# Four neighbouring tokens in a group: the layout of a routed-weight table, the stores that feed its stage, and the weights of the value pass

## The chip, the cores and the metric

The kernel runs on one core of a Trainium2 chip. The metric is the device time of one execution in microseconds, smaller is better. Matrix products run on TensorE (PE in the profile; PEld is its weight load), copies and element-wise work on VectorE (DVE), ScalarE (ACT) and GpSimd (POOL); SyncE (SP) only issues transfers.

## The reference, cut to what matters

A decoder block: attention and convolution side by side, a layer norm, and then an expert mixer in which the change lies. Each of 256 tokens has 8 heads that each pick 16 of 16,384 experts. An expert is one row of a table u and one row of a table v, 2048 numbers each:

```python
def block(yb):                      # PEER_BLOCK = 128 tokens
    ...                             # top-k over product keys: eidx [b, t, h, 16]
    g = jax.nn.softmax(top.astype(jnp.float32), axis=-1)
    u = u_tab[eidx]
    v = v_tab[eidx]
    h = jax.nn.gelu(jnp.einsum('btd,bthkd->bthk', yb, u))
    return jnp.einsum('bthk,bthkd->btd', g * h, v).astype(y.dtype)
```

The result is scaled, added to the residual and normalised once more.

## The kernel before, in words

The mixer does not gather all the rows. It computes the dot products of all tokens with all experts as matrix products over most of the columns (the other columns are gathered row by row), picks out the routed ones, and turns the routed weights back into a full matrix for a second matrix product.

- **The table W** is [128, 256, 128] fp32 in SBUF: partition p, token t, block j, for expert 128 j + p.
- **The u pass** (about 485 to 967 us) loops over 128 blocks. SP loads 128 rows of u (`u_load`, L1195), PE transposes them (ut, L1223), ScalarE and VectorE split them into a high and a low part (uh L1226, ul L1227), and PE adds three products (hi by hi, lo by hi, hi by lo: `mm3`, L290 to L292) into hp. ScalarE writes hp to W[:, :, j] (`u_keep`, L1474). Between these blocks run the `steps` of the routing, one or two pieces in each turn of the loop. The last of them is `feature_steps`: it forms features of the two key numbers (i1 and i2) of each routed slot, and stores them in bf16 to DRAM (feat, L1508). Each store goes out on ScalarE's queue, so it stands among the uh of the loop.
- **The x stage** (about 967 to 1148 us) works on groups of four tokens, 64 of them. Group q is the four tokens 32 apart, `group(t, q)`. The features of a group are loaded (L1545, L1554); small matmuls turn them into one-hot masks; `ext` (L1627) picks the 128 routed values of each token from W; GELU and the gates follow; and `sc` (L1674) makes, for each token, a 128 x 128 matmul that scatters the gated weights over partitions and blocks. The four matmuls of a group fill one PSUM bank, one quarter each, and `sc_keep` (L1682 on ScalarE, L1680 on VectorE) copies it over the group's part of W. Up to group 36 one group is scattered in each step, afterwards two in each.
- **The v pass** (about 1148 to 1645 us) loops over the 128 blocks j. W[:, :, j] is the weight matrix (stationary) and 1408 columns of the 128 rows of v are the moving matrix. Both are split into high and low parts: wh on ScalarE (L1720) and wl on VectorE (L1721), for two blocks at a time; vh (L1731) and vl (L1732) block by block. For each block PE makes 18 matmuls (`v_part`): three column pieces of 512, 512 and 384, two tiles of 128 tokens, and the three products of `mm3`. The other 640 columns are gathered for each token's own experts (gv, L1697 on GpSimd) and added up by VectorE (gacc, L1702).

Each engine works through its own list in order. The order of the x stage is written out by hand; that of the u and v pass follows the order of the calls. Each transfer that SP or ScalarE starts signals one of eight semaphores, in turn (DMAHW0 to DMAHW7), and waits for the transfer that used the semaphore before, unless that is known to have ended.

Of the kernel before, what the change touches and what calls it, by code (L numbers as in the profile page):

```python
# [9 lines left out]
F32R = mybir.dt.float32r  # L10
# [3 lines left out]
AF = mybir.ActivationFunctionType  # L14
# [5 lines left out]
P = 128  # L20
T = 256
# [54 lines left out]
def tile_hybrid_block(  # L76
# [6 lines left out]
    nc = tc.nc  # L83
    x, w_in, w_out, wq = x[0], w_in[0], w_out[0], wq[0]
# [3 lines left out]
    def dump(name, ap):  # L88
        if name in dbg:
            nc.sync.dma_start(dbg[name], ap)  # L90

    def flat3(t, a, b):
        return t[:, : a * b].rearrange("p (a b) -> p a b", b=b)
# [31 lines left out]
    raws, parts = {}, {}  # L125
# [163 lines left out]
    def mm3(acc, ah, al, bh, bl, start, stop):  # L289
        nc.tensor.matmul(acc, lhsT=ah, rhs=bh, start=start, stop=False)  # L290
        nc.tensor.matmul(acc, lhsT=ah, rhs=bl, start=False, stop=False)  # L291
        nc.tensor.matmul(acc, lhsT=al, rhs=bh, start=False, stop=stop)  # L292
# [650 lines left out]
    if True:  # L943
# [25 lines left out]
        for s in range(2):  # L969
            hi, lo = (stream.tile([P, 1024], F32R, name=f"{n}0_{'ab'[s]}", tag=n, bufs=HLB) for n in ("hi", "lo"))  # L970
            w = slice(s * 512, s * 512 + 512)
# [7 lines left out]
        for u in range(2):  # L979
            split_to(u)  # L980
            for j in range(4):
                i = j if u else (0, 2, 1, 3)[j]
# [139 lines left out]
    def gate_softmax(tt):  # L1122
        sh = [P, PH, TOPK]
        nc.vector.tensor_tensor(gs[:, tt], top[:, tt], top[:, tt, :, 0:1].to_broadcast(sh), op=OP.subtract)
        nc.scalar.activation(gs[:, tt], gs[:, tt], AF.Exp)
        nc.vector.tensor_reduce(gsum[:, tt, :, 0], gs[:, tt], axis=AX.X, op=OP.add)
        nc.vector.reciprocal(gsum[:, tt], gsum[:, tt])
        nc.vector.tensor_tensor(gs[:, tt], gs[:, tt], gsum[:, tt].to_broadcast(sh), op=OP.mult)

    def fl(t, tt):  # L1130
        return t[:, tt].rearrange("p a b -> p (a b)")
# [185 lines left out]
    if True:  # L1317
# [7 lines left out]
        i = nphase + 6  # L1325
# [41 lines left out]
        i = first_wq  # L1367
# [24 lines left out]
        for h in range(1, PH):  # L1392
            for half in range(2):
                p = 2 * h + half
# [37 lines left out]
        sp = scores.pop(PH - 1)  # L1432
# [22 lines left out]
    wpool = ctx.enter_context(ExitStack())  # L1455
    wp = wpool.enter_context(tc.tile_pool(name="wp", bufs=1, reuse_waits="tile"))
    W = wp.tile([P, T, P], F32, name="W")
    gbs = ctx.enter_context(ExitStack())
    rings.append([gbs.enter_context(tc.tile_pool(name="gb", bufs=GMORE, reuse_waits="tile")), GMORE, 0])
    wT, wv = gs.rearrange("p a b c -> p (a b c)"), hv  # L1460
    gT, ha = (t.rearrange("p a b c -> p (a b c)") for t in (i1, top))
    feats = [dram.tile([2, 5, P, P], BF, name=f"feat{n}") for n in range(2)]
# [10 lines left out]
    def u_keep(j):  # L1473
        nc.scalar.activation(W[:, :, j], hps.pop(j), AF.Copy)  # L1474

# [4 lines left out]
    def feature_steps():  # L1480
        dump("i1", i1)
        dump("i2", i2)
        for n, src in enumerate((i1, i2)):

            size = BIGM if n == 0 else 1.0
            v = src.rearrange("p a b c -> p a (b c)")
            sqf = tk.tile([P, 2, P], F32, name=f"fsq{n}", tag="oh", bufs=1)
            nc.vector.tensor_tensor(sqf, v, v, op=OP.mult)
            sqi = tk.tile([P, 2, P], U32, name=f"fsi{n}", tag="cand", bufs=1)
            nc.vector.tensor_copy(sqi, sqf)  # L1490
            yield
            for f in range(4):
                fr = tk.tile([P, 2, P], BF, name=f"fr{n}{f}", tag="scr", bufs=4)
                if f == 0:
                    nc.vector.memset(fr, size)
                elif f == 1:
                    nc.vector.tensor_scalar(fr, v, size, None, op0=OP.mult)
                else:
                    si = tk.tile([P, 2, P], U32, name=f"fi{n}{f}", tag="oh", bufs=1)
                    if f == 2:  # L1500
                        nc.vector.tensor_scalar(si, sqi, 7, 7, op0=OP.logical_shift_right,
                                                op1=OP.logical_shift_left)
                    else:
                        nc.vector.tensor_scalar(si, sqi, 127, None, op0=OP.bitwise_and)
                    nc.vector.tensor_scalar(fr, si, size, None, op0=OP.mult)
                yield
                for r in ((0, 1) if f == 0 else (f + 1,)):
                    nc.scalar.dma_start(feats[n][:, r].rearrange("a p c -> p a c"), fr)  # L1508
        for tt in range(2):
            gate_softmax(tt)  # L1510
            yield
        pt = psu.tile([P, 512], F32, name="colsg", tag="ut", bufs=4)
        for tt in range(2):
            nc.tensor.transpose(pt[:, tt * P:(tt + 1) * P], fl(gs, tt), ident)
        nc.scalar.activation(gT, pt[:, :T], AF.Copy)
        yield
# [13 lines left out]
        yield from feature_steps()  # L1530

    def group(t, q):
        tt, b = divmod(q, 32)
        return t[:, tt * P + b:(tt + 1) * P:32]

    NB = 4
    frow, bts = {}, {}
# [86 lines left out]
    def ext(q):  # L1624
        hot, wq_ = pts.pop(q), group(W, q)
        for j in range(4):
            nc.tensor.matmul(xps[q][:, j * P:(j + 1) * P], lhsT=hot[:, j], rhs=wq_[:, j],  # L1627
                             start=False, stop=j == 3)

    def ext_max(q):  # L1630
        nc.vector.tensor_reduce(group(ha, q), flat3(xps.pop(q), 4, P), axis=AX.X, op=OP.max)
# [32 lines left out]
    def sc_val(m, pair=False):  # L1664
        oas[m] = flat3((slots_[5], *more_slots, slots_[4], slots_[6])[m % 4] if pair else slots_[5 + m % 2], 4, P)
        ww, pp = group(wT, m), pos.pop(m)[1]
        wb = ww.rearrange("p (j o) -> p j o", o=1).to_broadcast([P, 4, P])
        nc.vector.scalar_tensor_tensor(oas[m], flat3(pp, 4, P), 0.0, wb, op0=OP.is_equal, op1=OP.mult)

    def sc(m, pair=False):  # L1670
        sp = (banks[4:6] + more_banks)[m % 4] if pair else banks[5]
        oh, oa = ohs.pop(m), oas.pop(m)
        for j in range(4):
            nc.tensor.matmul(sp[:, j * P:(j + 1) * P], lhsT=oh[:, j * P:(j + 1) * P], rhs=oa[:, j],  # L1674
                             start=True, stop=True)
        return sp

    def sc_keep(m, sp, vector=False):
        if vector:
            nc.vector.tensor_copy(group(W, m), flat3(sp, 4, P))  # L1680
        else:
            nc.scalar.activation(group(W, m), flat3(sp, 4, P), AF.Copy)  # L1682

    psv = ctx.enter_context(ExitStack())

# [1 line left out]
    raws, parts = {}, {}  # L1687
# [23 lines left out]
    nb = len(blocks)  # L1711
    halves_ = {}

    def v_rows(p, tt):
        if p not in halves_:
            halves_[p] = [vps[p % 2].tile([P, T, 2], F32R, name=f"w{x}{p}", tag=f"w{x}") for x in "hl"]
        s = slice(0, T) if tt is None else slice(tt * P, tt * P + P)
        wh, wl = (t[:, s] for t in halves_[p])
        src = W[:, s, 2 * p:2 * p + 2]
        nc.scalar.activation(wh, src, AF.Copy)  # L1720
        nc.vector.tensor_tensor(wl, src, wh.bitcast(F32), op=OP.subtract)  # L1721

    def v_cols(j, s, early=False):
        src, vhl = raws[j], parts.setdefault(j, [])
        if not vhl:
            vhl.extend(vps[j % 2].tile([P, VC], F32R, name=f"v{x}{j}", tag=f"v{x}") for x in "hl")
        vh, vl = (t[:, s] for t in vhl)
        if early:
            nc.gpsimd.tensor_copy(vh, src[:, s])
        else:  # L1730
            nc.scalar.activation(vh, src[:, s], AF.Copy)  # L1731
        (nc.gpsimd if early else nc.vector).tensor_tensor(vl, src[:, s], vh.bitcast(F32), op=OP.subtract)  # L1732

    def v_split(j):
        if j % 2 == 0:
            v_rows(j // 2, None)
        v_cols(j, slice(0, VC))

    def ahead_jobs():
# [72 lines left out]
    if True:  # L1812
# [41 lines left out]
        for q in range(QP, NQ + 1):  # L1854
            m = q - LAG
# [30 lines left out]
            if m >= 0:  # L1886
                sc_keep(m, sc(m))
# [4 lines left out]
        for m in range(NQ - QP, NQ, 2):  # L1892
# [12 lines left out]
            for p, sp in zip((m, m + 1), sps):  # L1905
                sc_keep(p, sp, p % 2 == 1)
            if m == NQ - 12:
                v_raw(2)
                v_rows(0, 0)
# [5 lines left out]
            if m == NQ - QP + 2:  # L1915
# [5 lines left out]
                vps = [psv.enter_context(tc.tile_pool(name="vp0", bufs=1, reuse_waits="tile", side="right"))]  # L1921
# [6 lines left out]
    if stop == "u":  # L1928
        dump("hv", hv)
        if "H" in dbg:  # L1930
            nc.sync.dma_start(dbg["H"], W)
        return
# [4 lines left out]
    acc = [[psv_.tile([P, 512], F32, name=f"f{tt}{b}", tag=f"f{tt}{b}")[:, :e - a]  # L1937
            for b, (a, e) in enumerate(blocks)]
           for tt in range(2)]
# [4 lines left out]
                v_sum(j, tt, nc.vector)  # L1944

    def v_part(j, tt, b, stop=False):
        (wh, wl), vhl = halves_[j // 2], parts[j]
        (a, e), s = blocks[b], slice(tt * P, tt * P + P)
        mm3(acc[tt][b], wh[:, s, j % 2], wl[:, s, j % 2], vhl[0][:, a:e], vhl[1][:, a:e], j == 0, stop)

    def v_use(j, tts=range(2)):
        for b in range(nb):
            for tt in tts:
                v_part(j, tt, b)
# [11 lines left out]
    if True:  # L1966
        v_rows(0, 1)
        for j in range(P):
# [7 lines left out]
            elif len(z2) < 2:  # L1976
                tt = len(z2)
# [113 lines left out]
```

## Time and profile before

| | |
|---|---|
| median of 3 runs | 1669.9 us |
| lowest to highest | 1668.81 to 1670.19 us |
| the profiled execution | 1661.9 us |
| its span in the profile | 1660.1 us |
| mean granted TensorE clock | 0.993 |
| TensorE busy | 1621.2 us, 98% of the span |
| VectorE, GpSimd, ScalarE busy | 87%, 53%, 49% |
| transfers | 475.19 MB, mean 286 GB/s |

Times inside the profile are in microseconds from the start of the span. A row of the groups gives line, engine, operation, tiles and shape, the count, then busy time, the mean of one in ns, and the idle time ahead of it with what ended it. A row of the timeline gives start, length and the instruction; ACTq and SPq are the queues on which ScalarE and SyncE issue transfers. A matmul's length holds its way through the array, so the distance of two starts tells how long the array is taken by one.

### The profile page before, as it was taken

The numbers are of one execution on the slowest core, as the hardware profiler recorded it, in microseconds if no ns is written. First come the engines' busy times: TensorE is split into PE (matmuls) and PEld (weight loads), VectorE is DVE, ScalarE is ACT, GpSimd is POOL, SyncE is SP. The second block draws the span as 40 slices with busy tenths as digits, with TensorE's granted clock in tenths as the row PEclk, the third lists the DMA queues.
The fourth block names the chain that finished last, engine by engine and source line by source line (L and its number), as shares of the span: only waits on it lengthen the run. The fifth ranks groups of instructions, "written<-read, shape, count | busy, mean of one in ns | idle before, by whom it ended". The sixth has DMA issues, their size and how long they took to land.

```text
span 1660.1 us, 30619 instructions
## 1 busy us (share of the span) xinstructions
PE 1621.2 (98%) x11627; PEld 1499.5 (90%) x11627; DVE 1451.2 (87%) x2660; ACT 812.9 (49%) x1260; POOL 887.0 (53%) x653
## 2 busy tenths in 40 slices
PE   9999999999999999999999999989999999999996
PEld 8998989988999999999999997878888888888884
DVE  6999667756899999999999879978889899898998
ACT  4444766645334444444444546867444444444442
POOL 0885000064573333333333347857887877777773
PEclk9999999999999999999999999999999999999998
DMA  9774435366658999999999988765999999999997
GB/s 286 228 230 142 154 111 189 102 222 197 215 186 313 353 349 351 350 353 344 352 348 354 360 314 270 253 208 183 336 363 365 349 354 348 351 350 353 350 352 263
DMA packets 178349, 475.19 MB, mean 286 GB/s; under 512 B 18305, under 2 KB 86425, under 8 KB 177945
## 3 DMA queue, kind: packets, MB, share of 16 engines
q1 hardware_dynamic: 117188, 253.62, 45.0%
q0 software_dynamic: 57488, 218.66, 35.9%
q8 instruction: 91, 1.49, 0.4%
q10 hardware_dynamic: 3524, 0.95, 0.2%
q14 instruction: 58, 0.47, 0.1%
HBM read 468.32 MB, written 4.85 MB: 285 GB/s over the span
## 4 chain that ended last, share of the span: by engine, by line
PE 54%; POOL 18%; issue 12%; DVE 9%; DMA 4%; ACT 2%; POOLq 0%; DVEq 0%; SPq 0%; ACTq 0%
POOL gv L1697 16%; PE hp L292 6%; PE hp L290 6%; PE hp L291 6%; PE ut L1223 6%; PE bank L1674 3%; DMA gv<-in_peer_v_dram,e 2%; DVE taps L483 2%; PE bank L1627 2%; PE pwq L292 1%; PE pwq L291 1%; PE pwq L290 1%; DVE gu L1166 1%; PE mixa L290 1%; PE pq L290 1%
## 5 line engine op out<-in xcount | busy, mean ns | idle before, releaser
L1697 POOL DMA_INDIRECT gv<-in_peer_v_dram,e x256 | 397.1, 1551 | 109.4 <-DVE gacc L1702 65.2
L1155 POOL DMA_INDIRECT gu<-in_peer_u_dram,eu x206 | 195.5, 949 | 318.2 <-DVE gu L1166 224.7
L290 PE MATMUL hp<-yh,uh 128*128 128x256 f32 x1024 | 310.4, 303 | 0.4 <-ACT W L1474 0.3
L1731 ACT ACTIVATE vh<-vr 128x1408 fp32r<-128x1408 f32 x127 | 175.6, 1382 | 274.4 <-DVE gacc L1702 244.0
L292 PE MATMUL hp<-yh,ul 128*128 128x256 f32 x1024 | 290.2, 283 | 0.9 <-DVE ul L1227 0.9
L291 PE MATMUL f<-vl,wh 128*128 128x512 f32 (+1 forms) x768 | 288.2, 375 | 2.1 <-DVE vl L1732 2.1
L291 PE MATMUL hp<-yl,uh 128*128 128x256 f32 x1024 | 289.3, 282 | 0.0
L290 PE MATMUL f<-vh,wh 128*128 128x512 f32 (+1 forms) x768 | 288.2, 375 | 0.8 <-ACT vh L1731 0.8
L292 PE MATMUL f<-vh,wl 128*128 128x512 f32 (+1 forms) x768 | 287.8, 375 | 0.0
L1226 ACT ACTIVATE uh<-ut 128x512 fp32r<-128x512 f32 x256 | 152.7, 598 | 255.2 <-PE ut L1223 249.9
L251 POOL TENSOR_TENSOR lo<-raw,hi 128x1024 fp32r<-128x1024 f32 (+1 forms) x77 | 173.0, 2262 | 144.6 <-ACT hi L233 138.4
L1732 DVE TENSOR_TENSOR vl<-vr,vh 128x1408 fp32r<-128x1408 f32 x127 | 206.3, 1624 | 46.2 <-ACT vh L1731 44.7
L1166 DVE SCALAR_TENSOR_TENSOR gu<-gu,yp 128x1024 f32<-128x1024 f32 x196 | 232.6, 1211 | 1.7 <-DMA gu<-in_peer_u_dram,eu 1.5
L233 ACT ACTIVATE hi<-raw 128x1024 fp32r<-128x1024 f32 (+1 forms) x137 | 141.4, 1036 | 148.0 <-PE pcg L291 29.1
L1702 DVE SCALAR_TENSOR_TENSOR gacc<-gv,hv,gacc 128x640 f32<-128x640 f32 x246 | 206.6, 878 | 4.0 <-DMA gv<-in_peer_v_dram,e 4.0
L292 PEld LDWEIGHTS hp<-yh,ul 128*128 128x128 f32 x1024 | 195.5, 191 | 1.4 <-DVE ul L1227 1.3
L290 PEld LDWEIGHTS hp<-yh,uh 128*128 128x128 f32 x1024 | 196.0, 191 | 0.8 <-ACT W L1474 0.8
L291 PEld LDWEIGHTS hp<-yl,uh 128*128 128x128 f32 x1024 | 196.5, 192 | 0.0
L1227 DVE TENSOR_TENSOR ul<-ut,uh 128x512 fp32r<-128x512 f32 x256 | 166.8, 681 | 15.3 <-ACT uh L1226 14.5
L291 PEld LDWEIGHTS f<-vl,wh 128*128 128x128 f32 x768 | 148.5, 193 | 24.2 <-DVE vl L1732 3.5
L290 PEld LDWEIGHTS f<-vh,wh 128*128 128x128 f32 x768 | 148.5, 193 | 21.8 <-ACT vh L1731 1.2
L292 PEld LDWEIGHTS f<-vh,wl 128*128 128x128 f32 x768 | 148.7, 194 | 19.9
(412 smaller groups left out, 3548.8 us busy)
## 6 DMA issues: line engine op xcount, KB each, us to landing
vr<-in_peer_v_dram SPq DMA_DIRECT2D x128, 704.0 KB
ur<-in_peer_u_dram SPq DMA_DIRECT2D x128, 512.0 KB
raw<-in_w_in_dram SPq DMA_DIRECT2D x32, 1024.0 KB
raw<-in_w_out_dram SPq DMA_DIRECT2D x16, 1024.0 KB
raw<-in_peer_wq_dram SPq DMA_DIRECT2D x15, 1024.0 KB
gv<-in_peer_v_dram,e POOLq DMA_INDIRECT x256, 7.5
gu<-in_peer_u_dram,eu POOLq DMA_INDIRECT x206, 7.8
raw<-in_w_in_dram SPq DMA_DIRECT2D x4, 608.0 KB
```

The costliest lines, as they stand in the source:

```text
L251: e.tensor_tensor(lo[:, a:b], src[:, a:b], hi[:, a:b].bitcast(F32), op=OP.subtract)
L290: nc.tensor.matmul(acc, lhsT=ah, rhs=bh, start=start, stop=False)
L291: nc.tensor.matmul(acc, lhsT=ah, rhs=bl, start=False, stop=False)
L292: nc.tensor.matmul(acc, lhsT=al, rhs=bh, start=False, stop=stop)
L1155: nc.gpsimd.indirect_dma_start(out=gt, out_offset=None, in_=ug, in_offset=bass.IndirectOffsetOnAxis(ap=fl(eu, tt)[:, c:c + 1], axis=0))
L1166: nc.vector.scalar_tensor_tensor(gt, gt, 1.0, yr, op0=OP.mult, op1=OP.mult, accum_out=hv[:, tt, c:c + 1])
L1226: nc.scalar.activation(uh, pt, AF.Copy)
L1227: nc.vector.tensor_tensor(ul, pt, uh.bitcast(F32), op=OP.subtract)
L1697: nc.gpsimd.indirect_dma_start(out=gvs[j, tt], out_offset=None, in_=v_tab, in_offset=bass.IndirectOffsetOnAxis(ap=fl(e4, tt)[:, j:j + 1], ...
L1702: engine.scalar_tensor_tensor(gacc[:, tt], gvs.pop((j, tt)), wv[:, tt, j:j + 1], gacc[:, tt], op0=OP.mult, op1=OP.add)
L1731: nc.scalar.activation(vh, src[:, s], AF.Copy)
L1732: (nc.gpsimd if early else nc.vector).tensor_tensor(vl, src[:, s], vh.bitcast(F32), op=OP.subtract)
```

## The change: four neighbours in a group, kept side by side

A group now is the tokens 4q to 4q+3. Inside its part of W, from the scatter on, the order is block first and token second, so that the 256 weights of one block lie in pieces of four in a row, one piece in each group. The pieces of the edit:

- The stores of the features are cut in four, each with every fourth partition (token) of the tile, so that token 4b+i comes to the place 32 i + b that the loads of the x stage expect.
- `sc` writes each of its four results with a distance of four elements in PSUM; `sc_keep` copies the bank as it is.
- `v_rows` splits one block at a time, into tiles that are contiguous over the 256 tokens, where it split two blocks and left them side by side in pairs. `v_part` takes its weights from them without a stride.

```diff
+    Wq = W.rearrange("p (q t) e -> p q (t e)", t=4)
...
                 for r in ((0, 1) if f == 0 else (f + 1,)):
-                    nc.scalar.dma_start(feats[n][:, r].rearrange("a p c -> p a c"), fr)
+                    for i in range(4):
+                        nc.scalar.dma_start(feats[n][:, r, i * 32:i * 32 + 32].rearrange("a b c -> b a c"), fr[i::4])
...
     def group(t, q):
-        tt, b = divmod(q, 32)
-        return t[:, tt * P + b:(tt + 1) * P:32]
+        return t[:, 4 * q:4 * q + 4]
...
         for j in range(4):
-            nc.tensor.matmul(sp[:, j * P:(j + 1) * P], lhsT=oh[:, j * P:(j + 1) * P], rhs=oa[:, j],
+            nc.tensor.matmul(sp[:, j::4], lhsT=oh[:, j * P:(j + 1) * P], rhs=oa[:, j],
                              start=True, stop=True)
...
     def sc_keep(m, sp, vector=False):
+        w = Wq[:, m]
         if vector:
-            nc.vector.tensor_copy(group(W, m), flat3(sp, 4, P))
+            nc.vector.tensor_copy(w, sp)
         else:
-            nc.scalar.activation(group(W, m), flat3(sp, 4, P), AF.Copy)
+            nc.scalar.activation(w, sp, AF.Copy)
...
-    def v_rows(p, tt):
-        if p not in halves_:
-            halves_[p] = [vps[p % 2].tile([P, T, 2], F32R, name=f"w{x}{p}", tag=f"w{x}") for x in "hl"]
-        s = slice(0, T) if tt is None else slice(tt * P, tt * P + P)
-        wh, wl = (t[:, s] for t in halves_[p])
-        src = W[:, s, 2 * p:2 * p + 2]
+    def v_rows(j, tt):
+        if j not in halves_:
+            halves_[j] = [vps[j % 2].tile([P, T], F32R, name=f"w{x}{j}", tag=f"w{x}") for x in "hl"]
+        s = slice(0, T // 4) if tt is None else slice(tt * P // 4, tt * P // 4 + P // 4)
+        wh, wl = (t.rearrange("p (q t) -> p q t", t=4)[:, s] for t in halves_[j])
+        src = Wq[:, s, 4 * j:4 * j + 4]
...
     def v_split(j):
-        if j % 2 == 0:
-            v_rows(j // 2, None)
+        v_rows(j, None)
         v_cols(j, slice(0, VC))
...
-        (wh, wl), vhl = halves_[j // 2], parts[j]
+        (wh, wl), vhl = halves_[j], parts[j]
         (a, e), s = blocks[b], slice(tt * P, tt * P + P)
-        mm3(acc[tt][b], wh[:, s, j % 2], wl[:, s, j % 2], vhl[0][:, a:e], vhl[1][:, a:e], j == 0, stop)
+        mm3(acc[tt][b], wh[:, s], wl[:, s], vhl[0][:, a:e], vhl[1][:, a:e], j == 0, stop)
```

The change moves instructions in ScalarE's list at two places. In the u pass, this is the first step that stores features (feat is the table in DRAM, fr the tile; uh are the high parts that PE's products of the loop need, W the results it leaves). Before:

```order
L1474 ACTIVATE W<-hp_11653 128x256
L1508 DMA feat_6004<-fr_11691 128x2x128 [waits DMAHW5_49,DVE_49]
L1508 DMA feat_6004<-fr_11691 128x2x128 [waits DMAHW6_49]
L1226 ACTIVATE uh_0_11756<-ut_0_11751 128x512 [waits PE_49,Activation_49]
L1226 ACTIVATE uh_1_11778<-ut_1_11773 128x512 [waits DVE_49,PE_49]
L1474 ACTIVATE W<-hp_11704 128x256
L1508 DMA feat_6004<-fr_11747 128x2x128 [waits DMAHW0_49,DVE_49]
```

And of the change:

```order
L1475 ACTIVATE W<-hp_11653 128x256
L1510 DMA feat_6004<-fr_11691 32x2x128 [waits DMAHW5_49,DVE_49]
L1510 DMA feat_6004<-fr_11691 32x2x128 [waits DMAHW6_49]
L1510 DMA feat_6004<-fr_11691 32x2x128 [waits DMAHW7_49]
L1510 DMA feat_6004<-fr_11691 32x2x128 [waits DMAHW0_49]
L1510 DMA feat_6004<-fr_11691 32x2x128 [waits DMAHW1_49]
L1510 DMA feat_6004<-fr_11691 32x2x128 [waits DMAHW2_49]
L1510 DMA feat_6004<-fr_11691 32x2x128 [waits DMAHW3_49]
L1510 DMA feat_6004<-fr_11691 32x2x128 [waits DMAHW5_49]
L1226 ACTIVATE uh_0_11762<-ut_0_11757 128x512 [waits PE_49,Activation_49]
L1226 ACTIVATE uh_1_11784<-ut_1_11779 128x512 [waits DVE_49,PE_49]
L1475 ACTIVATE W<-hp_11704 128x256
```

Two stores ahead of the next uh became eight, and the eighth waits for the same semaphore as the first, DMAHW5, which the first store signals; DMAHW4 is left out, having gone to a load of SP in between.

In the v pass, ScalarE's list of the high parts (wh of the weights, vh of the rows of v, for the block after the one that PE works on). Before:

```order
L1720 ACTIVATE wh_14745<-W 128x512
L1731 ACTIVATE vh_14749<-vr_14709 128x1408 [waits DMAHW4_49,DVE_49,PE_49]
L1731 ACTIVATE vh_14779<-vr_14739 128x1408 [waits DMAHW5_49,DVE_49,PE_49]
L1720 ACTIVATE wh_14809<-W 128x512
L1731 ACTIVATE vh_14813<-vr_14773 128x1408 [waits DMAHW6_49,DVE_49,PE_49]
L1731 ACTIVATE vh_14843<-vr_14803 128x1408 [waits DMAHW7_49,DVE_49,PE_49]
```

And of the change:

```order
L1722 ACTIVATE wh_15374<-W 128x256 [waits DVE_49,PE_49]
L1733 ACTIVATE vh_15378<-vr_15334 128x1408 [waits DMAHW3_49,DVE_49,PE_49]
L1722 ACTIVATE wh_15408<-W 128x256 [waits DVE_49,PE_49]
L1733 ACTIVATE vh_15412<-vr_15368 128x1408 [waits DMAHW4_49,DVE_49,PE_49]
L1722 ACTIVATE wh_15442<-W 128x256 [waits DVE_49,PE_49]
L1733 ACTIVATE vh_15446<-vr_15402 128x1408 [waits DMAHW5_49,DVE_49,PE_49]
```

A wh of half the size now stands ahead of each vh, and it waits for PE itself, where before it stood ahead of every second vh and waited for nothing. VectorE's wl and vl follow in the same manner.

## The prediction, made before the changed kernel ran

> **What bounds the kernel now.** I read the page first (slices, then the chain of waits), then the groups with shapes kept apart, then the timeline of one block of the value pass, then the windows and the chain in the stages that the edits touch.
>
> ```profile
> span 1660.1 us, 30619 instructions
> PE 1621.2 (98%) x11627; PEld 1499.5 (90%) x11627; DVE 1451.2 (87%) x2660; ACT 812.9 (49%) x1260; POOL 887.0 (53%) x653
> PEclk9999999999999999999999999999999999999998
> POOL gv L1697 16%; PE hp L292 6%; PE hp L290 6%; PE hp L291 6%; PE ut L1223 6%; PE bank L1674 3%; DMA gv<-in_peer_v_dram,e 2%; DVE taps L483 2%; PE bank L1627 2%; PE pwq L292 1%; PE pwq L291 1%; PE pwq L290 1%; DVE gu L1166 1%; PE mixa L290 1%; PE pq L290 1%
> ```
>
> TensorE has work for 98% of the span at full clock. The chain names the gathers of the value pass (gv L1697) with 16%, so that pass must be read itself. Two pieces of the chain there, with the pass's first matmul, and three windows:
>
> ```profile
> 1147.81 0.25 PE f L290
> ...
> 1178.07 6.65 DMA gv<-in_peer_v_dram,e
> ...
> 1212.92 7.92 DMA gv<-in_peer_v_dram,e
> ```
> ```profile
> 1200.00:1286.00 86.00, 86.00 (x404) 75.22 (x403) 77.39 (x78) 37.52 (x34) 69.33 (x46) 1.00 0.98 363
> 1300.00:1400.00 100.00, 100.00 (x470) 87.52 (x470) 90.02 (x91) 43.50 (x40) 78.82 (x51) 1.00 0.97 351
> 1500.00:1600.00 100.00, 100.00 (x470) 87.55 (x469) 90.03 (x90) 43.45 (x40) 79.71 (x51) 1.00 0.97 352
> ```
>
> The columns behind the sum are the busy times of PE, PEld, DVE, ACT and POOL, then granted clock, DMA share, GB/s. Early in the pass the transfers set the pace: gathers are on the chain to about 1221 us, and 363 GB/s moved. From 1300 us PE is never idle and 351 GB/s are enough. PE's own interval there, within one block:
>
> ```profile
> 1398.96 0.39 PE L290 MATMUL f<-vh,wh 128*128 128x512 f32 x1
> 1401.29 0.39 PE L291 MATMUL f<-vl,wh 128*128 128x512 f32 x1
> 1401.76 0.34 PE L290 MATMUL f<-vh,wh 128*128 128x384 f32 x1
> 1402.63 0.34 PE L292 MATMUL f<-vh,wl 128*128 128x384 f32 x1
> 1402.80 0.39 PE L290 MATMUL f<-vh,wh 128*128 128x512 f32 x1
> 1642.32 0.39 PE L292 MATMUL f<-vh,wl 128*128 128x512 f32 x1
> 1644.42 0.39 PE L292 MATMUL f<-vh,wl 128*128 128x512 f32 x1
> ```
>
> Between 1398.96 and 1401.29 lie ten starts: 0.233 us for 512 columns. Five 384-column starts take 0.87: 0.174 us each. A block is 12 and 6 of these, 3.84 us. At 1642 us, with ScalarE and GpSimd done, it is still 0.233 (2.10 over nine), so the interval belongs to the matmul and not to its neighbours.
>
> **The value pass.** The change makes the weights of these matmuls contiguous. Contiguous weights with 512 columns stand in another stage of this kernel:
>
> ```profile
> 366.00 0.39 PE L292 MATMUL mixb<-hi,cl 128*128 128x512 f32 x1
> 367.81 0.39 PE L291 MATMUL mixb<-lo,ch 128*128 128x512 f32 x1
> 470.73 0.28 PE L290 MATMUL pwq<-yh,hi 128*128 128x256 f32 x1
> 470.85 0.28 PE L291 MATMUL pwq<-yl,hi 128*128 128x256 f32 x1
> L292 PEld LDWEIGHTS f<-vh,wl 128*128 128x128 f32 x768 | 148.7, 194 | 19.9
> L292 PEld LDWEIGHTS mixb<-hi,cl 128*128 128x128 f32 x64 | 12.0, 188 | 2.5
> ```
>
> Eight starts in 1.81 us are 0.2265 us, 6.7 ns below 0.233; the loads take 188 ns against 194. If the stride is the cause, 128 blocks of 12 such matmuls gain 1536 x 6.7 ns = 10.2 us, 0.08 us a block (3.84 to 3.76). At 384 columns nothing is gained: 0.12 at 256 and 0.2265 at 512 make 0.173 by interpolation, and 0.174 is there already. The bounds are 0 and -10.2.
>
> The Trainium skill speaks against this gain: "SBUF — State Buffer" (Door 1, the note on cachelines) has full speed as long as a 16-byte line is hit twice, which a stride of two fp32 does; by that rule this term is 0. The rows at 512 columns differ from it by 6.7 ns, those at 384 don't.
>
> Can the others follow at 3.76? A block moves 704 KB of rows and two gathers of 128 x 640 fp32, 1.38 MB. Recorded 351 GB/s at 3.84 become 359 at 3.76, and 363 were moved early: enough, but the early blocks gain nothing. From 1147.8 to 1221 us these are 19 of 128, and 19 x 0.08 = 1.5 us of the 10.2 is lost. ScalarE and VectorE:
>
> ```profile
> L1731 ACT ACTIVATE vh<-vr 128x1408 fp32r<-128x1408 f32 x127 | 175.6, 1382 | 274.4 <-DVE gacc L1702 244.0 <-PE f L292 29.5 <-issue 0.8
> L1720 ACT ACTIVATE wh<-W 128x512 fp32r<-128x512 f32 x63 | 41.9, 665 | 0.0
> L1720 ACT ACTIVATE wh<-W 128x256 fp32r<-128x256 f32 x2 | 0.9, 427 | 0.5 <-DVE W L1680 0.5
> L1732 DVE TENSOR_TENSOR vl<-vr,vh 128x1408 fp32r<-128x1408 f32 x127 | 206.3, 1624 | 46.2 <-ACT vh L1731 44.7
> 1149.10 0.43 DVE L1721 TENSOR_TENSOR wl<-W,wh 128x256 fp32r<-128x256 f32 x1 [0.56 <-ACT wh L1720]
> 1399.16 1.38 ACT L1731 ACTIVATE vh<-vr 128x1408 fp32r<-128x1408 f32 x1 [1.89 <-DVE gacc L1702]
> ```
>
> Half-sized wh and wl take 0.43 each, and every block has one of each. The wait for PE that now stands at wh is the one that vh had; behind it are vh, vl and PE's second matmul. vh began 0.2 us into the block; now wh does: vh ends at 0.2 + 0.43 + 1.38 = 2.0, vl 1.62 later at 3.63, and PE needs it at 3.76 + 0.23 = 3.99. So 0.36 us of slack hides it; without that cover it would be about 0.1 us a block, 12 us. VectorE's 90% of 3.84 is 3.46, plus 0.43 - 0.34 makes 3.55 of 3.76. The start stands open: block 1's own pair of 0.43 us comes into it, where it was part of block 0's; I take 0.3. Term: -10.2 + 1.5 + 0.3 = -8.4.
>
> **The scatter.** The matmuls of L1674 now write each fourth PSUM element, and no matmul of this trace writes so.
>
> ```profile
> L1674 PE MATMUL bank<-slot,slot 128*128 128x128 f32 x512 | 68.0, 283 | 1.2 <-ACT W L1682 1.2
> 1120.03 1.98 PE bank L1674 x16
> ...
> 1122.34 1.98 PE bank L1674 x16
> L1682 ACT ACTIVATE W<-bank 128x512 f32<-128x512 f32 x46 | 27.6, 600 | 18.2 <-PE bank L1674 18.0
> ```
>
> Sixteen passes stand on the chain with 1.98 us, 0.124 for 128 columns, the length that a 256-column matmul of the other stages has (0.12). Each column has two slots here, so a write at half rate would fit under it. The other bound is a doubling: 512 x 0.112 to 0.124 us, +57 to 63 (28 if one pass in two doubles). A gain is excluded: no write was ever waited for. I take 0, by the half rate. The copies of L1682 (and L1680 on VectorE, one of each in a pair of groups) now read and write 512 elements in a row, where before four tokens' rows lay apart; at twice the 600 ns one still fits in the pair's 2.31 us, so they are nothing.
>
> "PSUM — Partial Sum Buffer" of the Trainium skill (Specifications, the row on cachelines) says that any non-contiguous access slows matmuls significantly; no run here shows it yet. By it this term is the upper bound.
>
> **The feature stores.** Ten stores become forty, on ScalarE's queue, in the middle of the u pass, where PE is never idle.
>
> ```profile
> 899.20 0.41 ACTq L1508 DMA_DIRECT2D feat<-fr  x1
> 899.64 0.48 ACTq L1508 DMA_DIRECT2D feat<-fr  x1
> 901.07 0.60 ACT L1226 ACTIVATE uh<-ut 128x512 fp32r<-128x512 f32 x1 [0.81 <-PE ut L1223]
> ...
> 927.29 0.60 ACT L1226 ACTIVATE uh<-ut 128x512 fp32r<-128x512 f32 x1 [0.81 <-PE ut L1223]
> 930.26 1.28 ACT L1125 ACT_TABLE_LOAD   x1
> 933.16 1.06 ACT L1226 ACTIVATE uh<-ut 128x512 fp32r<-128x512 f32 x2
> 934.09 0.60 PE L1223 MATMUL ut<-ident,ur 128*128 128x128 f32 x4
> 936.33 0.60 PE L1223 MATMUL ut<-ident,ur 128*128 128x128 f32 x4
> L1508 ACTq DMA_DIRECT2D feat<-fr x10: 366/388/484, 899.2 to 929.2; - x10
> ```
> ```profile
> q10 hardware_dynamic: 28, 0.01, 0.8%
> q10 hardware_dynamic: 358, 0.09, 7.1%
> q10 hardware_dynamic: 511, 0.12, 8.0%
> ```
>
> Twice (i1, i2) a step has eight stores ahead of the next uh, six times four. A loop of the u pass takes 3.75 us and splits two uh. Eight issues of 0.39 from 899.20 end at 902.3, which alone makes uh 1.25 late. But by the order the eighth store waits on the semaphore of the first, DMAHW5. The three rows are the stores' packets in the windows from 899 us to 903, 904.5 and 906: a quarter store has 64 packets, through between 903 and 904.5, about 903.3; both old stores (512) were through at 906.0. The first quarter's semaphore can't come before the one, and I bound it above by the other. So uh starts between 903.7 and 906.4 instead of 901.07, 2.6 to 5.3 late. What PE bears: after the table load uh came at 933.16 where 927.29 + 3.75 was due, 2.1 late, and the step on PE took 2.24 instead of 1.87, 0.37 lost; so about 1.8 is borne. Two bursts cost 2 x (0.8 to 3.5), in the middle 4.3. The other six (four issues, 1.6 us, in ScalarE's 0.81 + 1.21 us of idle per loop) and the loads of the u table on SyncE's queue (L1195), some of which wait on the stores' semaphores, I estimate at 1.2 together, at most 0.6 us a step. Term +5.5, bounds 0 and +11. Queued behind the waiting store are uh, ul, and PE's hp matmuls.
>
> **Sum.** -8.4 + 0 + 5.5 = -2.9 on the profiled execution's 1661.9. The median shown is 1669.9, 0.5% above that execution; the terms count stalls and intervals, so I carry the difference over: 1667.
>
> **Rivals.**
> - *The stores are hidden* (semaphores early, uh less than 1.8 late): -8.4 alone, 1661.5. For it: the old stores cost nothing visible. Against it: the packets' first 4 us.
> - *The interval isn't the stride's.* For it: 384 columns with the same stride pay nothing, and 194 ns of load fit in 233. Against it: two stages with the same instruction and 6.7 ns between them. Then the stores' wait remains: +5.5 + 0.3, 1675.7, slower; it decides where the pass gains less than some 2 us, since 1669.9 + 5.8 - 2 is over the bound of 3.3. By the rule of "SBUF — State Buffer" in the Trainium skill, above, this is the case that comes.
> - *The strided PSUM write slows the scatter.* It decides as soon as a pass takes over 0.124 us; one pass in two doubled is 1667 + 28 = 1695, both 1725. For it: nothing in the trace is written so. Against it: the half rate. The Trainium skill's "PSUM — Partial Sum Buffer" stands on this rival's side.
>
> **How the numbers follow.** Below 0.2%, 3.3 us, this kernel's runs can't be told from no change. The forecast has 0.42 (own range 1662 to 1673: faster 0.19, same 0.19, slower 0.04), the hidden stores 0.12 (faster), the interval 0.26 (same 0.09, slower 0.17), the scatter 0.20 (slower). Faster 0.31, same 0.28, slower 0.41. The range goes from 1660.5, just under the second case, to 1690, which takes in a mild scatter and leaves out its doubled passes.
>
> **What would show it.** The f matmuls of 512 columns start every 0.227 us, and a block takes 3.76 from 1300 us on, at about 359 GB/s; 0.233 shows the second rival. L1675's sixteen passes stay at 1.98 us, or the third is right. Around 900 and 918 us a uh several us late and an interval of the ut transposes above 1.87 show the stores; without it the first rival holds. vl later than PE's second matmul, or gathers on the chain past 1300 us, would prove the cover wrong.

## The result: slower by 0.6%

| | before | changed |
|---|---|---|
| median of 6 runs each | 1669.47 us | 1677.46 us |
| lowest to highest | 1665.79 to 1670.35 | 1676.9 to 1682.38 |
| the profiled execution | 1661.9 us | 1678.8 us |

The ratio is 1.0064, 95% interval 1.0052 to 1.0077: 8.7 to 12.9 us lost; the two medians of the table lie 8.0 us apart, a little under that. 1667 was forecast, a small gain. The two profiled executions lie further apart, 16.9 us, because that of before is 7.6 us under its own median; most of that lies in its short x stage (below).

First the page of the changed kernel: the span, the engines, and the chain by lines.

```profile
span 1677.0 us, 30971 instructions
PE 1627.9 (97%) x11627; PEld 1500.3 (89%) x11627; DVE 1456.2 (87%) x2724; ACT 816.1 (49%) x1324; POOL 883.2 (53%) x653
POOL gv L1699 9%; PE hp L290 6%; PE hp L292 6%; PE hp L291 6%; PE ut L1223 6%; PE f L291 3%; PE f L292 3%; PE f L290 3%; PE bank L1628 3%; PE bank L1675 3%; DVE taps L483 2%; PE pwq L292 1%; PE pwq L291 1%; PE pwq L290 1%; DMA gv<-in_peer_v_dram,e 1%
```

The chain's shares of lines don't tell where the time went: the gathers halved (16% to 9%), and nothing got faster by it. The stages do. They are measured between starts on PE's timeline: the first and the last hp matmul (u pass), from there to the first f matmul (x stage), and the first and the last f matmul of the loop's products (v pass). The last column is from that start to the end of the span.

| profiled execution | u pass | x stage | v pass | end |
|---|---|---|---|---|
| before | 481.3 | 164.9 | 498.0 | 14.6 |
| changed | 494.9 | 169.3 | 497.9 | 13.2 |
| difference | +13.6 | +4.4 | -0.1 | -1.4 |

The end by itself is no matter of the change: the kernel before has 14.6 us there in one execution and 13.1 in another (below). It goes with the last blocks of the v pass, so these two columns are read together below.

**The u pass** lost 13.6 us in this execution. ScalarE's timeline at the first burst of stores (ACTq: its queue issuing; seven transfers in a row stand in one row):

```profile
899.30 0.60 ACT L1226 ACTIVATE uh<-ut 128x512 fp32r<-128x512 f32 x1 [1.28 <-PE ut L1223]
899.37 0.70 ACTq L1510 DMA_DIRECT2D feat<-fr  x1
899.80 0.64 ACT L1475 ACTIVATE W<-hp 128x256 f32<-128x256 f32 x1
900.11 6.84 ACTq L1510 DMA_DIRECT2D feat<-fr  x7
907.05 0.60 ACT L1226 ACTIVATE uh<-ut 128x512 fp32r<-128x512 f32 x1 [6.62 <-DMA feat<-fr]
```

The uh that was due at about 901.2 comes at 907.05, after 6.62 us without work on ScalarE, which the profile puts down to the landing of a store. Of the seven transfers in one row, the last two taken alone are:

```profile
903.48 0.61 ACTq L1510 DMA_DIRECT2D feat<-fr  x1
906.37 0.58 ACTq L1510 DMA_DIRECT2D feat<-fr  x1
```

The seventh store of the burst is issued by 904.09. The eighth starts 2.28 us later: that is the wait for a semaphore, by the order DMAHW5, which the first store signals. PE's timeline behind it, and the windows (columns as before; the one behind the five engines' times is the granted clock):

```profile
904.29 0.60 PE L1223 MATMUL ut<-ident,ur 128*128 128x128 f32 x4
...
908.69 0.58 PE L290 MATMUL hp<-yh,uh 128*128 128x256 f32 x1 [3.81 <-ACT W L1475]
909.07 0.42 PE L291 MATMUL hp<-yl,uh 128*128 128x256 f32 x1
909.29 0.41 PE L292 MATMUL hp<-yh,ul 128*128 128x256 f32 x1
...
911.42 1.05 PE L1223 MATMUL ut<-ident,ur 128*128 128x128 f32 x4
```
```profile
900.00:910.00 10.00, 6.19 (x48) 5.95 (x48) 5.42 (x9) 2.13 (x5) 1.88 (x2) 0.84 0.97 334
910.00:915.00 5.00, 5.00 (x30) 5.00 (x30) 3.12 (x9) 1.60 (x3) 0.94 (x1) 0.63 0.55 168
```

PE stood still for 3.81 us. After that its matmuls start every 0.21 us instead of 0.12 until 913.5: the granted clock is 0.50 from 908.7 to 913.5, and 0.63 in the window shown. The transposes are 7.13 us apart instead of 1.87, and the step after takes 2.91 instead of 1.87, so one burst costs 6.3 us. The second burst (the transposes at 929.31 and 936.31 us, and 2.47 us for the step after) costs 5.7. A third place is the last step of four stores. ScalarE there:

```profile
941.97 3.63 ACTq L1510 DMA_DIRECT2D feat<-fr  x3
945.63 1.28 ACT L1125 ACT_TABLE_LOAD   x1 [3.22 <-issue]
946.92 0.31 ACT L1125 ACTIVATE gs<-gs 128x128 f32<-128x128 f32 x1
947.14 1.07 ACT L1226 ACTIVATE uh<-ut 128x512 fp32r<-128x512 f32 x2
```

Three of the four stores take 3.63 us, and the table load, which stood behind one store before, comes on top of them: a step of 4.02 us instead of 1.87, and 0.2 in the next, 2.4 in all. Together 14.4 us of late steps, of which before had 0.6 (its table load at 930 us).

**The v pass** took nearly as long as before, although its weights are contiguous now. The weight load is 188 ns, as it was in the mix stage (the mixb rows of the prediction), where before it was 194. The group of the loads, and the starts of the pieces of one block:

```profile
L292 PEld LDWEIGHTS f<-vh,wl 128*128 128x128 f32 x768 | 144.4, 188 | 20.2
```
```profile
1401.09 0.39 PE L290 MATMUL f<-vh,wh 128*128 128x512 f32 x1
...
1403.85 0.33 PE L290 MATMUL f<-vh,wh 128*128 128x384 f32 x1
...
1404.91 0.39 PE L290 MATMUL f<-vh,wh 128*128 128x512 f32 x1
```

The twelve of 512 columns take 2.76 us, 0.230 each, where 0.2265 was expected and 0.233 was. The six of 384 columns take 1.06, 0.177 each, where they took 0.174. So the wide ones gained 3 ns and not 6.7, the narrow ones lost 3, and a block is 3.82 to 3.83 us instead of 3.84.

That is 1.7 us in 128 blocks, and the pass is that far ahead after its first 120 (460.9 us from its start, before 462.6). It is lost again in the last but one block, where PE waits twice for about a microsecond in both kernels, and the changed one then runs at a lowered clock. A window behind these waits, before and changed:

```profile
1638.00:1642.00 4.00, 4.00 (x16) 2.70 (x15) 4.00 (x9) 0.00 (x0) 0.00 (x0) 1.00 0.92 314
1654.00:1658.00 4.00, 4.00 (x13) 3.53 (x12) 4.00 (x8) 0.00 (x0) 0.00 (x0) 0.57 0.81 290
```

This comes and goes whatever the kernel: that block takes 6.3 us in this profile of before, 7.9 in its second (below) and 8.0 here, and where it is short the end is 14.3 to 14.6 us, else 13.0 to 13.8. So the pass and the end have to be added: 512.6 us before, 511.1 changed, a gain of 1.5, where the two executions of before differ by 1.1.

**The x stage.** The strided write costs nothing where PE runs through. The chain of the changed kernel, sixteen passes of the scatter in a pair:

```profile
1140.70 1.98 PE bank L1675 x16
1143.01 1.98 PE bank L1675 x16
```

1.98 us, and 2.31 from pair to pair, are the numbers of before. The +4.4 us lie in single steps. The first of the runs shows that the kernel before has as much from one execution to the next.

### The profile page after: what moved, and what is told of

It reads as the page before. It is cut to its first block, busy times and chain, and to the rows that moved or that the text cites. A ratio compares the mean times of both kernels' runs of the same rounds, so it can differ in the third digit from the quotient of the medians.

```text
span 1677.0 us, 30971 instructions
## 1 busy us (share of the span) xinstructions
PE 1627.9 (97%) x11627; PEld 1500.3 (89%) x11627; DVE 1456.2 (87%) x2724; ACT 816.1 (49%) x1324; POOL 883.2 (53%) x653
## 4 chain that ended last, share of the span: by engine, by line
PE 65%; POOL 11%; DVE 10%; issue 9%; DMA 3%; ACT 2%; ACTq 0%; POOLq 0%; SPq 0%; DVEq 0%
POOL gv L1699 9%; PE hp L290 6%; PE hp L292 6%; PE hp L291 6%; PE ut L1223 6%; PE f L291 3%; PE f L292 3%; PE f L290 3%; PE bank L1628 3%; PE bank L1675 3%; DVE taps L483 2%; PE pwq L292 1%; PE pwq L291 1%; PE pwq L290 1%; DMA gv<-in_peer_v_dram,e 1%
## 5 line engine op out<-in xcount | busy, mean ns | idle before, releaser
L1699 POOL DMA_INDIRECT gv<-in_peer_v_dram,e x256 | 392.5, 1533 | 113.5 <-DVE gacc L1704 66.6
L1722 ACT ACTIVATE wh<-W 128x256 fp32r<-128x256 f32 (+1 forms) x129 | 53.7, 417 | 269.5 <-PE f L291 266.3
L291 PEld LDWEIGHTS f<-vl,wh 128*128 128x128 f32 x768 | 144.5, 188 | 26.6 <-DVE vl L1734 3.6
L290 PEld LDWEIGHTS f<-vh,wh 128*128 128x128 f32 x768 | 144.7, 188 | 23.6 <-ACT vh L1733 1.3
```

The costliest lines, as they stand in the source:

```text
L1699: nc.gpsimd.indirect_dma_start(out=gvs[j, tt], out_offset=None, in_=v_tab, in_offset=bass.IndirectOffsetOnAxis(ap=fl(e4, tt)[:, j:j + 1], ...
```

## The experiments

All ran beside runs of the kernel before on the same chip. The median of these differs from one set of runs to the next (1666.5, 1662.2 and 1664.1 us), so ratios are what counts. Three of the experiments have a single run and no interval.

### The kernel before, once more

No edit.

> The kernel before, unchanged, for a second profile. Its first profiled execution took 1661.9 us where the median of its runs is 1669.5. If the x stage's stalls come with the change, this profile shows the x stage at 164.9 us from the last hp to the first f matmul, as before; if they come and go in any execution, it can be 166 to 170. The u pass (first to last hp) should be 481 to 484 and the value pass 498.

Measured: 1670.05 us; u pass 481.2, x stage 171.9, v pass 500.6, end 13.1. The x stage is above the 166 to 170 that were expected. So the kernel before can have an x stage of 171.9 us: 7.0 more than in its first profile, more than the changed kernel's 169.3. Its chain shows a late load of features and passes that take longer behind it:

```profile
1113.72 8.31 DMA fsc<-feat
...
1123.41 3.33 PE bank L1674 x16
...
1127.07 1.98 PE bank L1674 x16
```

Sixteen passes take 3.33 us behind the wait, at a granted clock of 0.58, and 1.98 after that. In all eleven profiles of this section and the two above the x stage lies between 163.4 and 174.6 us, with the longest and the shortest of them in kernels with the new scatter. No part of it can be put down to the change, and a single profile's x stage tells nothing of 7 us. The u pass, on the other hand, is 481.1 to 481.6 us in every kernel with ten stores.

### The stores alone

The kernel before with the two hunks of the diff that cut the stores and change `group` (stores in four, groups of neighbours), with the old scatter and the old v pass.

> Only the stores in four and the groups of four neighbours; the scatter and the value pass as before. Theory (the stores make the whole loss): u pass 494 to 496 us instead of 481, and 8 to 14 us slower in all, as slow as the full change. Rival (the x stage or the new value pass carries part of the loss): less than 6 us slower.

Measured: 1.007, 1.005 to 1.009; u pass 493.0, a microsecond under what was expected, v pass 498.7. The stores by themselves lose as much as the whole change.

### One store again

```diff
-    feats = [dram.tile([2, 5, P, P], BF, name=f"feat{n}") for n in range(2)]
+    feats = [dram.tile([5, 2 * P, P], BF, name=f"feat{n}") for n in range(2)]
...
-                    for i in range(4):
-                        nc.scalar.dma_start(feats[n][:, r, i * 32:i * 32 + 32].rearrange("a b c -> b a c"), fr[i::4])
+                    nc.scalar.dma_start(feats[n][r].rearrange("(x b) c -> b x c", b=32), fr)
...
-            src = feats[n][tt].rearrange("f (j b) c -> (f j) b c", j=4)
+            src = feats[n].rearrange("f (j a b) c -> a (f j) b c", j=4, a=2)[tt]
```

(and the same view in `hot_load`.)

> The full change, but each feature store is one transfer again (ten in all): the table of features in DRAM is laid out with the four places of a group outside and the two token tiles inside, so that one transfer of three dimensions can write it. Theory: u pass back to 481 to 483, no wait above 2 us of ScalarE's queue near 900 us, value pass 498 as in the change, so 0 to 2 us from the kernel before. Rival (the strided PSUM write or the order of W costs in the x stage): 3 to 5 us slower than before, with x still at 169.

Measured: 0.9994, 0.9982 to 1.0005; u pass 481.2, x stage 174.6, v pass 498.1. The profiled execution, 1670.06 us, is the slowest of the ten, so its long x stage says nothing of the others. With the stores whole, the rest of the change is worth at most 3 us of gain and 1 of loss.

### The stores apart

```diff
                 for r in ((0, 1) if f == 0 else (f + 1,)):
+                    if r == 1:
+                        yield
                     for i in range(4):
```

The second four of a burst go out one step of the loop later; no step has more than four.

> The full change, with the eight quarter stores of a first feature in two steps of the loop, four and four. Theory (the stall of the u pass is the wait of the eighth store for the semaphore of the first, and PE's lowered clock after it): no wait above 2 us of uh on the stores near 900 and 925 us, u pass 482 to 486 us instead of 494.9. Rival (the stores' own issue time, 0.6 us each, and their load on the queues): still 489 or more.

Measured in one run: 1666.3 us beside 1662.2 of the kernel before; u pass 484.4. ScalarE's timeline there:

```profile
899.56 0.70 ACTq L1512 DMA_DIRECT2D feat<-fr  x1
900.30 1.94 ACTq L1512 DMA_DIRECT2D feat<-fr  x3
902.35 0.60 ACT L1226 ACTIVATE uh<-ut 128x512 fp32r<-128x512 f32 x1 [1.72 <-issue]
...
903.87 3.37 ACTq L1512 DMA_DIRECT2D feat<-fr  x3
907.35 0.60 ACT L1226 ACTIVATE uh<-ut 128x512 fp32r<-128x512 f32 x1 [2.98 <-PE ut L1223]
```

Four stores take 2.64 us to issue and delay uh by about one. Of the u pass's loss 3.1 us remain with ten steps of four. With eight in a step three profiles show 10.3 to 13.6 (491.6 us in "Other widths" below, 493.0 and 494.9), so 7 to 10.5 go. The absence of a wait over 2 us that was expected did not hold: three stores still take 3.37 us at 903.87, of which 1.52 lie between the end of the first issue (904.48) and the start of the second (906.00), and ScalarE idles 2.98 us ahead of the uh behind them. Which transfer that issue waited for is not shown.

### Other widths in the v pass

```diff
-    blocks = [(a, min(a + 512, VC)) for a in range(0, VC, 512)]
+    blocks = [(0, 470), (470, 940), (940, VC)]
```

> The full change, with the 1408 columns of the value pass in pieces of 470, 470 and 468 instead of 512, 512 and 384. Theory (contiguous weights do start every N/2.4 + 13.3 ns, but after each change of the column count some six matmuls start late): 18 matmuls at 209.2 ns, a block of 3.77 us instead of 3.83, value pass 490, so 7 to 8 us below the full change. Rival (the mean rate of the array is limited whatever the widths, at 3.83 us a block): 212.7 ns each, no gain.

Measured: 1.0052, 1.0034 to 1.007, against the full change's 1.0064; u pass 491.6, v pass 495.7, block 3.80 us. The 7 to 8 us under the full change that were expected did not come. A block on PE's timeline:

```profile
1398.80 0.37 PE L290 MATMUL f<-vh,wh 128*128 128x468 f32 x1
1399.84 0.37 PE L292 MATMUL f<-vh,wl 128*128 128x468 f32 x1
1400.04 0.38 PE L290 MATMUL f<-vh,wh 128*128 128x470 f32 x1
1402.39 0.38 PE L292 MATMUL f<-vh,wl 128*128 128x470 f32 x1
1402.60 0.37 PE L290 MATMUL f<-vh,wh 128*128 128x468 f32 x1
```

Without the very unequal widths the starts are regular: eleven in 2.35 us at 470 columns (0.214 each), five in 1.04 at 468 (0.208). So the array's mean rate isn't fixed at 3.83 us a block, as the rival has it; but the gain is half of what was expected, since 470 columns start every 214 ns and not 209. I took this for steps of 16 cycles of the array, and tested that.

### Widths that are multiples of 16

The edit is the same with `[(0, 480), (480, 944), (944, VC)]`; in one run on the change with ten stores, in the other on the kernel before.

> The change with ten single stores, and the columns of the value pass in pieces of 480, 464 and 464, all multiples of 16 at offsets that are multiples of 16. With 470, 470 and 468 the matmuls started every 213.3 and 206.7 ns, which are 512 and 496 cycles of the array. Theory (the interval goes in steps of 16 cycles, 32 cycles above a width that is a multiple of 16, when neighbours are nearly as wide): 213.3 ns for 480, 206.7 for 464, a block of 3.76 us, value pass 488 to 490 us, 8 us below the kernel before. Rival (a mean limit of the array near 211 to 213 ns a matmul): a block of 3.80 us or more, 4 us or less.

> The kernel before, with weights at a stride of two, and the pieces 480, 464 and 464 alone. Theory (a strided weight costs 16 cycles more for every wide matmul): 220 ns for 480 and 213.3 for 464, a block of 3.88 us, slower than before by 5 us. Rival (the stride costs nothing by itself; the mixture of widths did): a block of 3.76 us, and the whole gain without the new layout, 8 us faster.

Measured: 0.9998 (0.9989 to 1.0008) with a block of 3.84 us, and 1.0015 (1.0004 to 1.0026) with a block of 3.85. The theory failed in both: three steady widths don't give 3.76, and strided weights don't give 3.88. In the first run the numbers of the rival came, 3.80 us or more and no gain; but the next run speaks against a limit on the mean as the reason. In the second the rival failed too. The starts of the first are uneven again, from 0.20 to 0.23 us at a resolution of 0.01. The rule of 16 cycles is dropped; what is left is that 470 beside 468 runs evenly and 480 beside 464 does not.

### One change of width in a block

```diff
-        for b in range(nb):
+        for b in (range(nb) if j % 2 == 0 else range(nb - 1, -1, -1)):
             for tt in tts:
                 v_part(j, tt, b)
```

on the change with ten stores. Each second block takes its pieces as 384, 512, 512, so two blocks' narrow pieces and two blocks' wide ones lie together.

> The change with ten single stores and the old pieces 512, 512 and 384, but each second block takes them in the reverse order, so that the column count changes once in a block and not twice. Theory (the late starts after a change of width are what takes the gain): half of the 0.07 us between 3.83 and 3.76 comes back, a block of 3.79 to 3.80 us. Rival (a limit on the mean rate): 3.83 as before.

Measured in one run: 1653.1 us, v pass 493.7; the block is 3.79 and 3.80 us in turn. The timeline shows the mechanism:

```profile
1399.45 0.33 PE L290 MATMUL f<-vh,wh 128*128 128x384 f32 x1
...
1400.52 0.33 PE L290 MATMUL f<-vh,wh 128*128 128x384 f32 x1
...
1401.56 0.39 PE L290 MATMUL f<-vh,wh 128*128 128x512 f32 x1
1401.79 0.40 PE L291 MATMUL f<-vl,wh 128*128 128x512 f32 x1
1402.02 0.40 PE L292 MATMUL f<-vh,wl 128*128 128x512 f32 x1
...
1403.64 0.39 PE L290 MATMUL f<-vh,wh 128*128 128x512 f32 x1
...
1406.81 0.39 PE L292 MATMUL f<-vh,wl 128*128 128x512 f32 x1
```

The first six narrow matmuls after a wide one take 1.07 us, the next six 1.04. The first nine wide ones after a narrow one take 2.08 us (0.231 each), the fourteen from 1403.64 on 3.17 (0.2265 each). With contiguous weights a matmul whose predecessors have another width starts late for some six to nine matmuls, and then settles. The mix stage of the kernel before had shown it already, at its first rows, which the prediction leaves out; there the width goes from 256 to 512:

```profile
341.49 0.28 PE L292 MATMUL mixa<-hi,cl 128*128 128x256 f32 x1
341.61 0.40 PE L290 MATMUL mixb<-hi,ch 128*128 128x512 f32 x1
...
343.00 0.39 PE L290 MATMUL mixb<-hi,ch 128*128 128x512 f32 x1
```

Six starts in 1.39 us, 0.232 each, where the rows of the prediction, from 366 us on, have 0.2265.

Timed, beside the order alone on the kernel before:

> The change with ten single stores and each second block in reverse order of its pieces, timed. Theory: the value pass is 4 us shorter than before (block 3.795 against 3.84 us), the rest unchanged, so 3 to 5 us faster, ratio 0.997 to 0.998. Rival (the 1653.1 of the single look is another gain, outside the value pass): 7 us or more faster.

> The kernel before with each second block in reverse order, and its strided weights. Theory (with the stride the 512-column matmuls take 233.3 ns also long after a change of width, so there is nothing for the order to save): block 3.84 us, no change in time. Rival (the order alone gives the gain, the stride has no part in it): 3.80 us, 4 us faster.

Measured: 0.9959 (0.9946 to 0.9972) with the new layout, 7 us, v pass 494.9; 0.9993 (0.9977 to 1.0008) with the strided weights, block 3.84 us, v pass 499.2. The order alone does nothing:

```profile
1400.53 0.39 PE L290 MATMUL f<-vh,wh 128*128 128x512 f32 x1
...
1402.62 0.39 PE L290 MATMUL f<-vh,wh 128*128 128x512 f32 x1
...
1405.89 0.39 PE L292 MATMUL f<-vh,wl 128*128 128x512 f32 x1
```

Nine starts of 512 columns in 2.09 us after the change of width, and fourteen in 3.27 behind them: 0.232 and 0.2335. With the stride there is no settling at 0.2265. So the stride does cost the 6.7 ns of the prediction, in a run of one width, and the mixture of widths took them back. The first run gained 4.7 to 9.0 us by the interval, where 3 to 5 were expected, so its rival's 7 or more isn't excluded by the time alone. The traces put the gain in the v pass: with the end it takes 508.0 us, where the two profiles of before have 512.6 and 513.7 and the order alone 513.8, while the u pass (481.5) and the x stage (166.3) are as in the other kernels with ten stores.

### The same without the new table

```diff
-            halves_[p] = [vps[p % 2].tile([P, T, 2], F32R, name=f"w{x}{p}", tag=f"w{x}") for x in "hl"]
+            halves_[p] = [vps[p % 2].tile([P, 2, T], F32R, name=f"w{x}{p}", tag=f"w{x}") for x in "hl"]
...
-        wh, wl = (t[:, s] for t in halves_[p])
+        wh, wl = (t.rearrange("p e t -> p t e")[:, s] for t in halves_[p])
...
-        mm3(acc[tt][b], wh[:, s, j % 2], wl[:, s, j % 2], vhl[0][:, a:e], vhl[1][:, a:e], j == 0, stop)
+        mm3(acc[tt][b], wh[:, j % 2, s], wl[:, j % 2, s], vhl[0][:, a:e], vhl[1][:, a:e], j == 0, stop)
```

with the reverse order of each second block, on the kernel before.

> The kernel before with the reverse order and with the split halves kept as [2, 256] per partition instead of [256, 2]: the reads of W, the groups, the stores and the scatter stay as before, only the writes of wh and wl go to two rows of 256, and the weights are contiguous. Theory (contiguous weights and one change of width in a block are all that the value pass needs): block 3.80 us as with the new table, 3 to 5 us faster than before. Rival (the split with its writes far apart gets slower, up to twice 0.67 us on ScalarE and VectorE, and vl comes late): waits of PE for vl, block 3.84 us or more.

Measured: 0.9961, 0.9949 to 0.9974, 1656.86 us beside 1664.14; block 3.80 us, v pass 491.6, 506.2 with the end: 6.4 to 7.5 us less than in the two profiles of before. It beats both kernels, as the version above does, with four edited lines. The split did get slower, as the rival has it:

```profile
L1720 ACT ACTIVATE wh<-W 128x512 fp32r<-128x512 f32 x63 | 72.7, 1154 | 0.0
L1721 DVE TENSOR_TENSOR wl<-W,wh 128x512 fp32r<-128x512 f32 x63 | 70.7, 1122 | 0.0
1300.00:1400.00 100.00, 100.00 (x475) 87.05 (x474) 94.55 (x91) 49.78 (x40) 79.46 (x51) 1.00 0.97 360
```

wh takes 1.15 us instead of 0.67 for a pair of blocks and wl 1.12 instead of 0.68, but VectorE has the room (94.6 of 100 us busy), and PE works through the window.

## Why the prediction was wrong

- **The value pass (-8.4 forecast, -1.5 in the traces with the end, -0.1 without).** The step that failed is "If the stride is the cause, 128 blocks of 12 such matmuls gain 1536 x 6.7 ns", with its companion "At 384 columns nothing is gained". The cause was right: contiguous weights bring 512 columns to 0.2265 us. The price was taken from the middle of a long run of one width and carried to a loop that changes the width twice in a block of 18. That "the interval belongs to the matmul and not to its neighbours" had been read with other engines idle, not with other widths. After each change the matmuls start late, together 0.07 us in a block, of the 0.08 that the stride had cost. The other engines were as forecast: vl is ready in time, wh beside vh hides, and transfers follow (352 GB/s at 3.83 us, and 358 where the block was 3.80). The start, put at 0.3 us, cost 0.4 to 0.7: the first eight blocks take 32.3 us, where the two profiles of before have 31.9 and 31.7.
- **The feature stores (+5.5 forecast, bounds 0 and +11; +13.6 in the traces).** The mechanism was right: the eighth store waits for a semaphore, and uh behind it. Its size was not. The eighth store starts at 906.37, where 906.0 was the upper bound of that semaphore, and its issue takes 0.58 us, not the 0.39 of a whole store; so uh came at 907.05, where 906.4 was the upper bound, and PE stood 3.8 us where a burst was put at 0.8 to 3.5. And what wasn't counted at all: behind the pause the array runs at half its clock (0.50 granted, 0.21 us a matmul), which costs another 2.5 us of the first burst. "The other six" steps were put, with the loads, at 1.2; the last of them alone made 2.4, of which before had 0.6, since its stores and the table load behind them added up. The same stores lost 11.7 and 10.3 us in two other profiles, so 13.6 is the upper end of three.
- **The scatter (0 forecast).** Right: 1.98 us for sixteen passes, 2.31 a pair. The half rate of these passes was the argument for it; that this is the reason was not tried. The Trainium skill's rule in "PSUM — Partial Sum Buffer" (Specifications), that any non-contiguous access slows matmuls significantly, isn't borne out by these rows: a distance of four elements left the pass at its length.
- **The rivals.** The second one, that nothing is gained in the pass and the stores' wait stays, gave 1675.7 us for 1677.46 measured. That it came so near is partly luck: it has the stores at 5.5 us, where they lost 10 to 14. Its reason was half right: not that the stride is free, as the rule of "SBUF — State Buffer" (Door 1) in the Trainium skill has it, which the steady 0.233 and 0.2265 contradict, but that another delay took its place. It had 0.26, behind the forecast's 0.42. Its first argument, "384 columns with the same stride pay nothing", holds in the steady rows as well (0.173 to 0.174 with the stride and without), and why is open. That 1677.46 lies in the stated range is luck too: the range reached up there for a mild slowing of the scatter, which did not come.
- **Own time and runs.** The sum stood on an execution 7.6 us below the median. The x stage of one and the same kernel differs by 7.0 us between two executions; a difference of stages is only worth what the stage repeats.

## What to carry to other kernels

An interval read in one stage is a price for another only if the instructions around it are alike: read the first matmuls after a change of shape as well as the middle of a run, and, where shapes must differ, put equal ones side by side. A transfer that is cut into pieces costs an issue and a semaphore for each piece; count how many a queue holds before the next waits for an earlier one to land, and what stands behind it. A pause of PE can cost more than its length: here 3.8 us of it, with the lowered clock behind, made 6.3. A stage's time should be read with what follows it, as the v pass with its end.

## What was not expected of the hardware

- With contiguous weights, the 512-column fp32r matmul starts every 0.2265 us in a long run, but 0.231 in the first nine after 384 columns and 0.232 in the first six after 256; 384 columns start every 0.177 in the first six after 512, and 0.173 after that. With weights at a stride of two it is 0.233 and 0.174, without a visible settling. Pieces of 470 and 468 run evenly at 0.214 and 0.208, pieces of 480 and 464 unevenly with 0.213 in the mean. Nothing here shows why.
- After PE had stood for 3.8 us, its matmuls started every 0.21 us instead of 0.12 for 4.8 us, at a granted clock of 0.50. Two waits of 0.90 and 1.16 us near the end of the v pass were followed by a granted clock of 0.57 in the changed kernel, and by none below 1.00 in the same place before (0.77 and 1.16).
- A store of 32 partitions at a distance of four mostly took 0.6 to 0.7 us to issue, where the store of all 128 took 0.39. The single store with its target in another order took 0.59 to 0.71, so the number of partitions alone doesn't set it.
